# A hybrid decoder layer on one core: the attention output's halves added on the vector engine, its turns and scalings staged, and filler, loads and splits spread

## The chip, the cores and the metric

The kernel runs on one core of a Trainium2 chip. A core has engines that run side by side, each with its own instruction queue in program order: TensorE (PE, matrix products; PEld is its load of the stationary operand), the vector engine (DVE), the scalar engine (ACT), GpSimd (POOL) and SyncE (SP, which here issues every DMA). Matrix products and transposes write to PSUM, which has eight banks of 128 x 512 fp32 values; the other operands lie in SBUF. The metric is the device time of one execution in microseconds, taken as the median over runs.

## The reference

One layer on x of 1024 tokens by 1024 columns, all in fp32:

```
h   = rmsnorm(x) * g_pre;  p = h @ W_in                      (1024 x 3584)
A   = attention, 8 heads of 64: three dilated windows (128,1), (512,4), (2048,16),
      mixed per position by their softmax denominators, ALiBi bias, causal
R   = HGRN2 recurrence, 4 heads of 128, per-head norm, output gate silu
x   = x + rmsnorm(concat[rmsnorm(A), R] @ W_out) * g_post
x   = x + rmsnorm(relu(rmsnorm(x) @ W1)^2 @ W2) * g_mlp_post  (4096 wide)
```

The mixture of the three windows is the same as one causal softmax whose bias has the logarithm of the number of windows that contain the key; this bias comes as a table for each head.

## The kernel before, in words

Products that need fp32 precision are made of three passes over pairs of reduced-precision values (`three_pass`, lines 86 to 89): every operand is split into a high part (an ACT copy, line 83) and a low part (a DVE subtraction, line 84). The order of all instructions on every engine is written out by hand.

**Recurrence.** After the first norm and turns (to about 45 us), `hgrn_core` runs for the four heads: a diagonal from `prod` (`pd`, line 379), seven levels of a chunk tree (`pl`, line 393), a state update, and the output `po` in two groups of four blocks (lines 434 to 446). These steps are too short for TensorE, so matmuls of the next projection are put between them.

**Filler.** A projection is a generator that yields a cost after each handful of matmuls (650 after three 128x512 ones, 330 after three 128x256 ones). `fill(ns)` runs the generators of a queue until that much cost is spent, and an overshoot is kept as a credit. `drain()` runs all that is left.

**Attention.** The eight heads are taken in four pairs. `attn_proj(pr)` makes q, v and k of a pair: two halves of 512 tokens each, 48 units of 650 and two of 450, 32,100 in all. For k it copies a high part (ACT), subtracts a low part (POOL, line 524) and copies both to the other 64 partitions by four DMAs for each half. There are 64 steps, (head, block b of 128 rows), b = 0 to 7. Step s issues: the exponentials of step s+1; the scores of step s+2 (`ps`, lines 563 and 564), with bias and row maximum on the DVE (line 566); the turns of step s (`pt`, line 590), split by ACT (line 593) and DVE (line 594); and after every second step `weigh` for a group of 256 rows.

`weigh` (from line 600) multiplies the stacked high and low halves of v with the turned probabilities. So the upper and lower 64 partitions of its bank `po` (tag `pv`, two banks; the trace says `pov`) hold two halves of the result which have to be added. ACT copies them to `ot`. One step later `finish` multiplies `ot` by `fold`, two 64 x 64 unit matrices on top of each other (line 618): one fp32 product adds the halves and turns them. The DVE then scales rows by the reciprocal denominators into `anat` (line 621). A pair's `anat` is stored to DRAM; the last pair's stays.

After the scores and turns a step asks for filler: `fill(2700.0 - 320.0 * b)`, in the last 16 steps 1300. The K part of the next pair waits until step 6 of the pair before it. Two steps ahead of a new pair (`fresh`) all that is left of the projection is drained, since the next scores need it.

**Bridge to the output projection.** `hooks` adds work to single steps. From 45: gain and the recurrence's rows of the first four blocks are loaded (`early_open`, `erows`, into blocks that hold the layer's input until the last projection is done), POOL multiplies them (line 658), TensorE turns them (`pmt`, line 698), and splits of W_out are made at steps 46 to 49. `early_out` then is filler. Rows of the attention part are loaded at 55, normed at 59 to 62.

**Output projection and second norm.** The loop over t = 0 to 7 makes the product with W_out, the residual and the second norm, and `next_turn(t - 2)` turns the result for the next layer; for t - 2 = 0 to 3 it also splits it (`h2`), ACT and DVE reading PSUM. After it come the two layers of the second half as Strassen-like products, which fill the time from about 660 us to the end.

## Time and profile before

| What | us |
|---|---|
| median of three runs | 1316.15 (1313.2 to 1319.82) |
| the profiled execution | 1313.2 |
| its span, first to last instruction | 1311.4 |
| PE busy | 1264.5 (96%) |
| DVE busy | 858.7 (65%) |
| ACT busy | 515.1 (39%) |
| POOL busy | 283.6 (22%) |

A row of a group has the line, engine, operation, output and inputs, shape and count; then the busy time, the mean of one instruction in ns, and the idle time of its engine just before. A row of waits has who waited for whom, the total, how often, and the longest. In the table of stretches the last three numbers are the granted TensorE clock (1.00 is full speed), the busy share of the DMA engines and GB/s. Ends of matmuls are modelled and overlap, so the pace is read from starts, not from durations.

### The profile page before, as it was taken

To read this page: it belongs to the slowest core of one execution; us is meant where nothing else is said; L and a number is where in the kernel's file an instruction comes from. 1 tells how busy PE (TensorE), PEld (TensorE's weight loads), DVE (VectorE), ACT (ScalarE), POOL (GpSimd) and SP (SyncE) were. 2 spreads that over 40 slices of the span, in tenths; PEclk is the share of its full clock that TensorE was granted. 3 is DMA by queue.
4 is the path that set the end of the run, shared out by engine and by line. 5 is a ranking of instruction groups with operands and counts; after the bars stand their busy time and mean duration, and the time that the engine had idled before them with its cause. 6 is when DMAs were issued, how large, how long until landed. Compare 5 with 4: busy or idle time off the path is not lost. (4 is left out here: it accounts for less than half of the span.)

```text
span 1311.4 us, 17500 instructions
## 1 busy us (share of the span) xinstructions
PE 1264.5 (96%) x6730; PEld 1081.8 (82%) x6730; DVE 858.7 (65%) x1431; ACT 515.1 (39%) x908; POOL 283.6 (22%) x276
## 2 busy tenths in 40 slices
PE   9999999999989999898999899999999999999997
PEld 8898989888878888786887688888887888888886
DVE  5556566675656655666757656666666777688956
ACT  6612121213545554564555422222234633344412
POOL 0000000012011111123432178755651000000002
PEclk9999999999999999899999899999999999999999
DMA  5202020213122222416251444534469453444423
GB/s 203 65 17 65 17 64 17 65 49 98 48 81 65 81 65 59 137 41 215 97 177 58 143 168 169 177 129 140 174 222 347 165 196 115 146 131 128 147 80 130
DMA packets 58563, 153.77 MB, mean 117 GB/s; under 512 B 5104, under 2 KB 13040, under 8 KB 58224
## 3 DMA queue, kind: packets, MB, share of 16 engines
q1 hardware_dynamic: 58480, 152.66, 34.9%
q8 instruction: 53, 0.87, 0.3%
q14 instruction: 30, 0.25, 0.1%
HBM read 106.50 MB, written 39.85 MB: 112 GB/s over the span
## 5 line engine op out<-in xcount | busy, mean ns | idle before, releaser
L88 PE MATMUL f<-bl,ah 128*128 128x512 f32 x392 | 152.6, 389 | 0.5 <-DVE bl L84 0.5
L87 PE MATMUL f<-bh,ah 128*128 128x512 f32 x392 | 152.6, 389 | 0.4 <-ACT acc L1441 0.4
L89 PE MATMUL f<-bh,al 128*128 128x512 f32 x392 | 152.5, 389 | 0.0
L84 DVE TENSOR_TENSOR al<-ar,ah 128x1024 fp32r<-128x1024 f32 x49 | 60.7, 1239 | 49.6 <-ACT ah L83 21.7
L88 PEld LDWEIGHTS f<-bl,ah 128*128 128x128 f32 x392 | 73.6, 188 | 16.1 <-DVE bl L84 0.8
L87 PEld LDWEIGHTS f<-bh,ah 128*128 128x128 f32 x392 | 73.6, 188 | 16.0 <-ACT acc L1441 0.9
L89 PEld LDWEIGHTS f<-bh,al 128*128 128x128 f32 x392 | 73.6, 188 | 15.3
L83 ACT ACTIVATE ah<-ar 128x1024 fp32r<-128x1024 f32 x49 | 52.3, 1067 | 54.1 <-PE f L89 25.3
L566 DVE CUSTOM_DVE_ANT_0 p<-ps,bt 128x512 f32<-128x512 f32 (+2 forms) x96 | 50.6, 552 | 31.7 <-PE ps L564 31.5
L1577 POOL TENSOR_SCALAR fp<-fss 128x1 f32<-128x1 f32 x8 | 3.5, 432 | 268.8 <-ACT fd L1574 268.8
L594 DVE TENSOR_TENSOR ptl<-pt,pth 128x512 fp32r<-128x512 f32 (+2 forms) x96 | 50.2, 551 | 16.4 <-ACT pth L593 16.3
L593 ACT ACTIVATE pth<-pt 128x512 fp32r<-128x512 f32 (+2 forms) x96 | 43.3, 486 | 42.0 <-PE pt L590 41.8
L590 PE MATMUL pt<-ident,p 128*128 128x128 f32 x288 | 43.6, 279 | 11.6 <-DVE ptl L594 11.6
L393 PEld LDWEIGHTS pl<-qt,kt 128*128 128x128 f32 x448 | 52.9, 192 | 1.5 <-PE pm_av L89 0.9
L393 PE MATMUL pl<-qt,kt 128*128 128x64 f32 x448 | 53.5, 272 | 0.5 <-DVE qt L399 0.5
L577 ACT ACTIVATE p<-p,nm 128x128 f32<-128x128 f32 (+3 forms) x64 | 49.5, 773 | 10.0 <-DVE nm L572 5.7
L524 POOL TENSOR_TENSOR kl<-kf,kh 64x512 fp32r<-64x512 f32 x16 | 20.4, 1274 | 151.3 <-ACT kh L523 150.7
L231 ACT ACTIVATE inat<-pig,rstd 128x128 f32<-128x128 f32 x32 | 11.6, 367 | 95.4 <-PE pig L89 82.3
L590 PEld LDWEIGHTS pt<-ident,p 128*128 128x128 f32 x288 | 33.7, 142 | 17.2 <-DVE ptl L594 14.2
L83 ACT ACTIVATE bh<-br 128x1024 fp32r<-128x1024 f32 x28 | 29.9, 1067 | 41.1 <-PE f L89 35.8
L79 POOL TENSOR_SCALAR ms<-hss 128x8 f32<-128x8 f32 x4 | 0.8, 196 | 203.6 <-DVE hss L445 203.6
L84 DVE TENSOR_TENSOR wl<-raw,wh 128x1024 fp32r<-128x1024 f32 x23 | 31.3, 1359 | 18.0 <-ACT wh L83 18.0
(1584 smaller groups left out, 3848.9 us busy)
## 6 DMA issues: line engine op xcount, KB each, us to landing
ar<-actd SPq DMA_DIRECT2D x49, 512.0 KB, 3.7
raw<-in_w_in_dram SPq DMA_DIRECT2D x28, 512.0 KB, 3.7
w1r<-in_w_ff_dram SPq DMA_DIRECT2D x14, 1024.0 KB, 6.5
br<-in_w_ff_dram SPq DMA_DIRECT2D x14, 1024.0 KB, 6.5
actd<-e SPq DMA_DIRECT2D x17, 768.0 KB, 4.2
actd<-e SPq DMA_DIRECT2D x11, 1024.0 KB, 4.1
xr<-in_x_dram SPq DMA_DIRECT2D x8, 512.0 KB, 9.0
bt<-in_bias_tab_dram SPq DMA_DIRECT2D x8, 512.0 KB, 4.3
```

The lines of the kernel that those rows point to most:

```text
L83: S.activation(hi, src, AF.Copy)
L84: eng.tensor_tensor(out=lo, in0=src, in1=f32(hi), op=ALU.subtract)
L87: TE.matmul(dst, lhs[0], rhs[0], start=start, stop=False)
L88: TE.matmul(dst, lhs[0], rhs[1], start=False, stop=False)
L89: TE.matmul(dst, lhs[1], rhs[0], start=False, stop=stop)
L393: TE.matmul(pl[:, n * 64:(n + 1) * 64], kt[:, n * P:(n + 1) * P], qv[:, n * nb:(n + 1) * nb, 1, :], start=True, stop=True)
L524: G.tensor_tensor(out=stacks[i]["kl"][a:b, sl], in0=full[a:b], in1=f32(stacks[i]["kh"][a:b, sl]), op=ALU.subtract)
L566: V.tensor_tensor_reduce(out=pe[:, k0:k0 + n], in0=pS[:, :n], in1=bts[hd][:, o:o + n], scale=1.0, scalar=-3.0e38, op0=ALU.add, op1=ALU.max ...
L577: S.activation(pe[:, :nk], pe[:, :nk], AF.Exp, bias=nm[:, b:b + 1], accum_out=dn[:, b:b + 1])
L590: TE.transpose(pt[:, j * P:(j + 1) * P], pe[:, jj * P:(jj + 1) * P], ident)
L593: S.activation(hi, src, AF.Copy)
L594: V.tensor_tensor(out=lo, in0=src, in1=f32(hi), op=ALU.subtract)
```

## The change

Six things, all between the recurrence and the second half.

1. *Halves.* `fold` and its load go. `weigh` has ACT copy one half of `po` straight into the 64 partitions of `anat` that belong to the head. `finish_step`, called once a step, moves a result through three stages: the DVE adds the other half from PSUM; for the second head of a pair, TensorE turns the two heads' 128 x 256 together by two transposes into the free half of the bank; the DVE scales by the reciprocals of both heads at once (`rd` now has a column for each head) back into `anat`.
2. *Filler in attention.* `3400 - 360 b` up to step 43, 1000 to step 47, 1300 after. A pair's projection counts as done before its last yield; at a `fresh` step only what the next scores need is run.
3. *Rows' load.* `early_rows` is called in the last pair's K projection after its first half. It loads rows and a separate copy of the gain; POOL's products move to steps 45 and 46, turns to 47 to 50, `early_out` starts at 48. The last head's bias table shares a tile with the gain. Norms and gains of the attention rows come at 61 to 63.
4. *Filler in the recurrence.* 4500 before `pd` become 2200 before and 2300 after it; 3000 after `po` become 1500 between the two groups and 1500 after.
5. *Second layer's input parts.* `next_turn` only copies; `split_tokens` splits two blocks at once from that copy in SBUF at t = 4 and t = 6.
6. W_out's second part takes slabs, the third the rotating buffers.

```diff
-        fill(4500 * scale)
+        fill(2200 * scale)
         pd = bank("t", f"pd{h}")
...
         cur = tot
+        fill(2300 * scale)
...
             pos.append(po)
+            if g4 == 0:
+                fill(1500 * scale)
...
-        fill(3000 * scale)
+        fill(1500 * scale)
...
+            if hf == 0 and pr == AH // 2 - 1:
+                early_rows()
             full = half(f"kf{pr}{hf}")
...
+            pairs[pr] = (stacks, vs)
             yield 650.0
-        pairs[pr] = (stacks, vs)
...
-        ot = sp.tile([P, 256], F32, tag="ot", name=f"ot{hd}_{g}", bufs=1)
-        S.activation(ot, po[:, :256], AF.Copy)
-        return po, ot
+        a, b = halves[hd % 2]
+        S.activation(turned_of(hd, g)[a:b], po[a:b, :256], AF.Copy)
+        return po
+    def finish_step(*new):
+        for hd, g, po in stages[2]:
+            scale_rows(hd, g, po)
+        for hd, g, po in stages[1]:
+            ft = turned_of(hd, g)
+            for u in range(2):
+                TE.transpose(po[:, 256 + u * P:256 + (u + 1) * P], ft[:, u * P:(u + 1) * P], ident)
+        for hd, g, po in stages[0]:
+            a, b = halves[hd % 2]
+            c, d = halves[1 - hd % 2]
+            o = turned_of(hd, g)[a:b]
+            V.tensor_tensor(out=o, in0=po[c:d, :256], in1=o, op=ALU.add)
+        stages[:] = [list(new), [x for x in stages[0] if x[0] % 2], stages[1]]
+    def scale_rows(hd, g, po):
-        for u in range(2):
-            TE.matmul(po[:, 256 + u * 64:256 + (u + 1) * 64], ot[:, u * P:(u + 1) * P], fold, start=True, stop=True)
-        for u in range(2):
-            b = 2 * g + u
-            V.tensor_scalar(anats[pr][:, b, hd % 2], po[:, 256 + u * 64:256 + (u + 1) * 64],
-                            stats[hd]["rd"][:, b:b + 1], None, op0=ALU.mult)
+        V.tensor_tensor(out=anats[pr][:, 2 * g:2 * g + 2], in0=po[:, 256:].rearrange("p (u i d) -> p u i d", u=2, i=2),
+                        in1=stats[hd]["rd"][:, 2 * g:2 * g + 2].unsqueeze(3).to_broadcast([P, 2, 2, 64]), op=ALU.mult)
...
+    def early_rows():
+        early["rows"] = wide.tile([P, NE, AW], F32, tag="A", name="erows")
+        early["table"] = wide.tile([P, 2, T], F32, tag="A", name="etable")
...
+        gains["early"] = early["table"][:, 1, :AW]
+        nc.sync.dma_start(out=gains["early"], in_=g_mix[:AW].partition_broadcast(P))
+        for q in range(NE // 2):
+            nc.sync.dma_start(out=early["rows"][:, 2 * q:2 * q + 2],
+                              in_=mix_dram[2 * q * P:2 * (q + 1) * P, :AW].rearrange("(n p) d -> p n d", p=P))
...
-            if th == 0:
-                hi, lo = (q[:, :, c:c + P] for q in h2[kh])
-                split_into(hi, lo, src)
+    def split_tokens(kh, c):
+        hi, lo = (q[:, :, c:c + 2 * P] for q in h2[kh])
+        split_into(hi, lo, hraw[kh, 0][:, :, c:c + 2 * P])
...
     hooks = {
-        45: lambda: [drain(), load_gain("gmix", "R", g_mix), early_open()],
-        46: lambda: w_get(WO0, 0),
-        47: lambda: [w_get(WO0 + 1, 0), row_rec(0), row_rec(1)],
-        48: lambda: [row_turn(0, 0), w_get(WO0 + 2, 0), row_rec(2), row_rec(3)],
-        49: lambda: [row_turn(1, 0), w_get(WO0 + 3, 0), queue.extend(early_out(t) for t in range(NE))],
-        50: lambda: row_turn(2, 0),
-        51: lambda: row_turn(3, 0),
+        45: lambda: [row_rec(0), row_rec(1)],
+        46: lambda: [w_get(WO0, 0), row_rec(2), row_rec(3)],
+        47: lambda: [row_turn(0, 0), w_get(WO0 + 1, 0), load_bias(AH - 1)],
+        48: lambda: [drain(), load_gain("gmix", "R", g_mix), early_sums(), w_get(WO0 + 2, 0), row_turn(1, 0),
+                     queue.extend(early_out(t) for t in range(NE))],
+        49: lambda: [w_get(WO0 + 3, 0), row_turn(2, 0)],
+        50: lambda: row_turn(3, 0),
...
-        59: lambda: [row_norm(0), row_gain(0)],
-        60: lambda: [row_norm(1), row_gain(1)],
-        61: lambda: [row_turn(0, 1), w_get(WO0 + 4, 0)],
-        62: lambda: [row_norm(2), row_gain(2), w_get(WO0 + 5, 0)],
-        63: lambda: w_get(WO0 + 6, 0),
+        61: lambda: [row_norm(0), row_gain(0), w_get(WO0 + 4, 0)],
+        62: lambda: [row_turn(0, 1), row_norm(1), row_gain(1), w_get(WO0 + 5, 0)],
+        63: lambda: [row_norm(2), row_gain(2), w_get(WO0 + 6, 0)],
     }
...
         if fresh and s + 2 < n_steps:
-            drain()
+            while pairs[(s + 2) // 16] is None:
+                fill(1.0)
             if (s + 2) // 16 + 1 < AH // 2:
+                drain()
                 queue.append(attn_proj((s + 2) // 16 + 1))
             look(s + 2)
...
-        fill(2700.0 - 320.0 * b if s < n_steps - 16 else 1300.0)
+        fill(3400.0 - 360.0 * b if s < n_steps - 20 else 1000.0 if s < n_steps - 16 else 1300.0)
...
+        if t in (4, 6):
+            for kh in range(2):
+                split_tokens(kh, (t - 4) * P)
```

## The prediction

> **What bounds the kernel now.** I read the page first (shares), then the table of stretches by stage, then TensorE's own waits, then the timeline round the longest of them, then the granted clock there.

> ```profile
> span 1311.4 us, 17500 instructions
> PE 1264.5 (96%) x6730; PEld 1081.8 (82%) x6730; DVE 858.7 (65%) x1431; ACT 515.1 (39%) x908; POOL 283.6 (22%) x276
> ```

> TensorE is the bound: 96% busy, the next engine 65%. So two things count: TensorE work that goes away, and the 47 us in which TensorE stands. The stages (stretch, length, busy time of PE, PEld, DVE, ACT, POOL, granted clock, DMA share, GB/s):

> ```profile
> 60.00:320.00 260.00, 258.61 (x1779) 238.36 (x1778) 160.06 (x288) 56.91 (x94) 18.41 (x16) 1.00 0.17 49
> 320.00:392.00 72.00, 64.94 (x386) 56.02 (x385) 44.90 (x143) 36.39 (x82) 10.21 (x8) 1.00 0.26 74
> 392.00:460.00 68.00, 64.14 (x377) 56.12 (x376) 40.50 (x131) 34.66 (x76) 10.26 (x8) 0.96 0.25 70
> 460.00:533.00 73.00, 65.35 (x381) 56.94 (x380) 39.73 (x131) 34.41 (x77) 12.30 (x10) 0.94 0.29 87
> 533.00:590.00 57.00, 55.76 (x348) 49.40 (x347) 39.27 (x119) 38.84 (x90) 10.82 (x18) 0.97 0.21 61
> 590.00:662.00 72.00, 67.01 (x330) 54.46 (x330) 49.66 (x69) 37.89 (x103) 27.42 (x57) 1.00 0.44 152
> ```

> TensorE stands 1.4 us in the recurrence (60 to 320), 7.1, 3.9 and 7.7 us in the first three attention pairs, 1.2 in the last, 5.0 in output projection and second norm (590 to 662). Its waits, over the whole run (total, times, longest, in us):

> ```profile
> PE pt L590 <- DVE ptl L594: 11.6, 7, 2.8
> PE pmt L698 <- POOL erows L658: 4.7, 1, 4.7
> PE ps L563 <- DVE mx L566: 2.3, 1, 2.3
> PE ph L785 <- DVE esum L775: 2.3, 1, 2.3
> PE pmt L698 <- DVE row L682: 1.5, 1, 1.5
> PE pmt L698 <- DVE ptl L594: 0.9, 1, 0.9
> PE pwo L87 <- ACT mt L83: 0.8, 1, 0.8
> ```

> In attention TensorE waits for the DVE to split the turned probabilities, although the DVE is busy 54 to 69% there: single steps are uneven, not the totals. The end of the second pair in the timeline:

> ```profile
> 449.18 0.69 DVE L521 TENSOR_TENSOR kf<-pm_ak,rrow 128x512 f32<-128x512 f32 x1 [4.75 <-PE pm_ak L89]
> 450.80 1.04 PE L590 MATMUL pt<-ident,p 128*128 128x128 f32 x8
> 451.68 0.56 PE L618 MATMUL pov<-fold,ot 128*128 128x64 f32 x4
> 452.30 2.00 DVE L84 TENSOR_TENSOR wl<-raw,wh 128x1024 fp32r<-128x1024 f32 x1 [2.04 <-ACT wh L83]
> 455.49 0.48 PE L590 MATMUL pt<-ident,p 128*128 128x128 f32 x1 [2.85 <-DVE ptl L594]
> ```

> The rest of the next pair's projection is drained in one lump; the DVE is idle for 4.75 us, then gets everything at once, and TensorE, whose filler is spent, stands 2.85 us. The clock answers to such places:

> ```profile
> 382.80:386.20 3.40, 1.89 (x16) 1.57 (x15) 1.85 (x1) 2.85 (x6) 2.40 (x2) 1.00 0.51 118
> 451.00:454.50 3.50, 1.64 (x14) 1.32 (x12) 2.20 (x2) 2.59 (x6) 2.14 (x2) 1.00 0.53 124
> 454.50:461.30 6.80, 5.81 (x22) 5.34 (x23) 2.83 (x13) 1.86 (x6) 0.00 (x0) 0.50 0.54 169
> 519.30:522.70 3.40, 1.47 (x13) 1.22 (x12) 1.33 (x4) 2.67 (x6) 2.26 (x2) 1.00 0.51 116
> 522.70:526.20 3.50, 3.50 (x18) 3.31 (x18) 2.92 (x12) 3.06 (x8) 0.00 (x0) 0.51 0.92 238
> 529.60:536.40 6.80, 4.12 (x17) 3.83 (x18) 2.09 (x2) 2.50 (x6) 4.96 (x4) 0.50 0.20 80
> ```

> After 3.4 us in which TensorE worked 1.64 or 1.47 us the clock is halved; after 1.89 us it is not. Half of what ran in such a stretch is lost: 2.9 us in the first, 2.1 in the last; the middle one ends in the 4.7 us wait for POOL anyway and costs nothing.

> **The change part by part.** Groups by shape within 320 to 590 that price it (busy us, mean ns, idle before):

> ```profile
> L594 DVE TENSOR_TENSOR ptl<-pt,pth 128x512 fp32r<-128x512 f32 x48 | 32.3, 687 | 14.0 <-ACT pth L593 14.0
> L566 DVE CUSTOM_DVE_ANT_0 p<-ps,bt 128x512 f32<-128x512 f32 x48 | 32.3, 686 | 27.9 <-PE ps L564 27.9
> L618 PE MATMUL pov<-fold,ot 128*128 128x64 f32 x128 | 18.6, 270 | 0.0
> L621 DVE TENSOR_SCALAR anat<-pov,rd 128x64 f32<-128x64 f32 x62 | 14.2, 271 | 0.0
> L610 ACT ACTIVATE ot<-pov 128x256 f32<-128x256 f32 x32 | 12.3, 384 | 20.4 <-PE pov L607 20.0
> L84 DVE TENSOR_TENSOR wol<-raw,woh 128x1024 fp32r<-128x1024 f32 x5 | 6.9, 1376 | 1.7 <-ACT woh L83 1.7
> L594 DVE TENSOR_TENSOR ptl<-pt,pth 128x256 fp32r<-128x256 f32 x16 | 6.7, 416 | 1.5 <-ACT pth L593 1.5
> ```

> *1, fold matmuls out.* 64 fp32 products with `fold` are 128 instructions. Four of them move TensorE's end from 451.84 to 452.24: 0.40 us, by 32 groups 12.8 us. In come 32 transposes (two for each pair of heads and group of 256 rows); the row of eight takes 1.04 us with its first latency, eight start before 451.68, so 0.11 us each: 3.5 us. Net -9.3; by the groups' busy time, which counts latency, 18.6 - 32 x 0.15 = 13.8 is the other end. I take -9.3, the pace, since TensorE works without a break there.

> *2, DVE and ACT of it.* Out: 64 scalings, 14.7 us. In: 32 additions of 64x256 and 16 scalings of 128x256 from PSUM, at the 416 ns of a 128x256 operation: 20.0 us. The DVE gets 5.3 us more over 270 us in which it idles over 100; hidden at the even steps, counted in the budgets below. ACT's 32 copies keep their length, with half the partitions. Queued behind the new DVE additions is only the next step's work; they run a step after the copy they need, so no new wait is seen. The store of a pair's output goes two steps later, past one weight load on SP, and is read four steps after at the earliest; the load of `fold` at the start goes: 0.

> *3, filling.* A projection is 32,100 units of cost. Steps ask for 25,280 a pair now (so some 6,800, ten units, go as the lump) and for 34,240 after, so the lump vanishes and the last two steps of a head get 1240 and 880 in place of 780 and 460. What waits instead: at the step with seven turns before a new pair the queue is empty. There the DVE has 2 x 686 + 687 + 416 + 2 x 416, with small ones 3.8 us, TensorE four score matmuls and six turns, 1.6: a wait of some 1.6 at two borders, since one step of slack lies before it. In the steps that carry splits of W_out (46 and 47, filler spent) the DVE has 3.3 (0.5 for a score, 687 and some 550 for turns, 0.15, 1376) and 5.1 (0.6, 2 x 687, 0.15, 2 x 416, 1376, and 687 for a row), TensorE 2.5 and 1.6: 4.2 of wait. The first steps have 0.8 us more filler against the 2.3 wait: 1.5 left. A half-clock stretch after step 47, chance one half: 1.5. Small ones in the middle of pairs: 1.1. After: 2 x 1.6 + 4.2 + 1.5 + 1.5 + 1.1 = 11.5. Before, from the rows above: 11.6 + 4.7 + 2.3 + 0.9 of waits and 5.0 of clock, 24.5. Net -13.0. Bounds: -24.5, if all waits go; +2, if each lump only becomes as long a wait elsewhere.

> *4, rows' load.* Rows and a copy of the gain are loaded as soon as the first half of the last K projection has read its blocks, before that half's four copies on the SP queue; POOL multiplies them at steps 45 and 46. The 4.7 wait is in part 3. What stands behind them on SP, the K copies, isn't needed for three steps: 0. `row_norm` and `row_gain` of rows 0 and 1 come two steps later, the first only a step before its turn; and at the end a turn takes a PSUM bank that the new scaling frees. I take +1.0 for both, between 0 and the 2.85 of the longest wait.

> *5, recurrence.* 2300 of the 4500 units before `pd` move behind it, half of the last 3000 between its two groups. What covers `prod`:

> ```profile
> 130.04 0.39 PE L89 MATMUL pm_f<-hTh,wl 128*128 128x512 f32 x1
> 130.26 0.28 PE L87 MATMUL pig<-wig2h,hTh 128*128 128x256 f32 x1
> 130.38 0.28 PE L88 MATMUL pig<-wig2l,hTh 128*128 128x256 f32 x1
> 132.95 0.69 DVE L369 TENSOR_TENSOR prod<-qt,kt 128x512 f32<-128x512 f32 x1
> ```

> `prod` ends 3.2 us after the last `pm_f`. 2200 units are seven of 330, each three matmuls at 0.12: 2.5 us. So `pd` waits 0.7 in three heads, 0.5 in the last (four units of 650 are 2.8 us): +2.7, where nothing is gained, because the stage stands 1.4 us in all. Bounds 0 to 3.

> *6, second layer's input parts.* Eight splits of 128x512 (half of them ACT, half DVE) leave the steps of t = 2 to 5, four of twice that length come at t = 4 and 6.

> ```profile
> 616.10 0.69 DVE L84 TENSOR_TENSOR h2l<-ph,h2h 128x512 fp32r<-128x512 f32 x1 [1.84 <-ACT h2h L83]
> 617.08 0.69 DVE L84 TENSOR_TENSOR h2l<-ph,h2h 128x512 fp32r<-128x512 f32 x1 [0.28 <-ACT h2h L83]
> 617.68 1.28 DVE L775 SCALAR_TENSOR_TENSOR esum<-xres,x2r,gmlp 128x1024 f32<-128x1024 f32 x1
> ```

> `esum`, for which TensorE then waits 2.3, is held by these two and their 1.84 and 0.28 of idling; without them it starts some 3 us earlier. The 2.3 and the 0.8 go: -3.1. The later lumps are two DVE operations of about 1.24, in steps without a TensorE wait above 0.4 us: 0. Bounds -5 to +2.

> Sum: -9.3 - 13.0 + 1.0 + 2.7 - 3.1 = -21.7. The profiled execution took 1313.2 us (span 1311.4), so 1291.5; it was the fastest of the three shown, 2.95 under their median, against which I forecast 1316.15 - 21.7, rounded 1294.

> [...] Row first: of the 1.64 us of work ahead of the first half-clock stretch, the eight turns that start at 450.80 are nearly 0.9. [...]

> **Rivals.**
> *A, the waits stay.* TensorE's saving falls in steps where it waits for the DVE, and parts 3 and 4 only move waits. For it: all 11.6 us of `pt` waits are for the DVE, whose work grows by 5.3. Against: the 4.75 idle before the 2.85 wait. Then -9.3 and about half of the clock loss, -2.5, remain: 1304.
> *B, the clock.* Turns and pauses together bring a half-clock stretch at each of four borders: 4 x 2.9 = 11.6 where I count 1.5: 10 later, 1304. For it: 1.64 us and 1.89 us lie close; against: the waits left are shorter. [...]
> *C, slower.* A PSUM bank of `pov` is now held until the third stage has scaled it, and two serve all. If each of the 16 held banks makes the next weighing wait for the DVE's queue, the change loses as soon as one costs over 21.7/16 = 1.36 us; at the 2.85 of the longest wait it gives +24, 1340. For it: the steps leave one step between scaling and reuse. Against: TensorE waits for the DVE at `pov` only 0.2 us now, and the scaling comes directly behind a split that it needs anyway.
> *D, nothing.* The lump was no loss, as the work must be done, and new waits on the additions eat the fold's 9.3: 1316.

> **How the numbers follow.** Forecast 0.62, A 0.16, B 0.08, C 0.06, D 0.08. The three runs lie 0.5% apart (6.6 us), about what can be told from no change. Faster by more: forecast, A, B, 0.86; same: D, 0.08; slower: C, 0.06. Range: part 3's lower bound reaches 1283; upward A and B with their 1304 and 5 us of spread, 1309; that leaves out D and C, and some of the bottom.

> **What would show it.** TensorE's busy time down by 9 to 14; in the attention stage no DVE idling of 4.7 before `kf`, `pt` waits under 6 in sum, no wait on `erows`; half-clock stretches there down from three to one at most. A new wait of `pd` on the DVE of 0.5 to 0.8 in each head. No `ph` wait on `esum`. Wrong would be: waits of `pov` for the scaling (C), `pt` waits as before at other steps (A), clock under 0.95 in every pair (B).

## The result, and the profile after

The changed kernel takes 1308.98 us in the median (1306.96 to 1309.98) against 1314.61 of the kernel before beside it. The ratio is 0.9946, with a 95% interval of 0.9930 to 0.9962: 5.6 us faster by the medians, where 21.7 were forecast. The profiled execution took 1308.3 us.

Its page, first lines (after):

```profile
span 1306.5 us, 17279 instructions
PE 1254.8 (96%) x6634; PEld 1070.6 (82%) x6634; DVE 866.9 (66%) x1411; ACT 518.7 (40%) x904; POOL 282.9 (22%) x276
```

TensorE's busy time fell by 9.7 us, as forecast (9 to 14), but the span by 4.9 only. To see where the rest went, both spans are cut at the same points of the work: the last `po` of the recurrence, the fifth step's first turn of the last head, the first `ph` turn, the first product of the second layer. The table of stretches of the kernel before (stretch, length, busy time of PE, PEld, DVE, ACT, POOL, granted clock, DMA share, GB/s):

```profile
0.00:316.31 316.31, 311.31 (x2124) 285.77 (x2125) 191.11 (x352) 94.30 (x176) 19.21 (x22) 1.00 0.20 64
316.31:571.33 255.02, 236.31 (x1390) 206.03 (x1389) 153.90 (x502) 133.73 (x297) 37.81 (x32) 0.97 0.26 75
571.33:607.32 35.99, 34.89 (x198) 29.70 (x196) 21.92 (x44) 21.63 (x55) 13.51 (x28) 1.00 0.54 181
607.32:671.84 64.52, 59.53 (x298) 48.57 (x296) 44.61 (x60) 32.65 (x89) 23.54 (x49) 1.00 0.32 111
```

The same of the changed kernel:

```profile
0.00:320.80 320.80, 313.67 (x2124) 287.63 (x2125) 190.82 (x352) 93.99 (x176) 18.70 (x22) 0.99 0.20 63
320.80:564.50 243.70, 225.61 (x1303) 194.11 (x1302) 160.35 (x485) 136.96 (x294) 37.60 (x30) 0.99 0.28 80
564.50:606.48 41.98, 34.90 (x188) 29.11 (x186) 23.62 (x45) 22.14 (x56) 15.58 (x29) 0.96 0.47 155
606.48:667.61 61.13, 59.24 (x298) 48.69 (x296) 44.72 (x56) 32.76 (x85) 21.31 (x49) 1.00 0.33 114
```

| Stretch | change of length, us | forecast |
|---|---|---|
| to the end of the recurrence | +4.5 | +2.7 |
| attention up to the last half head | -11.3 | about -21.4: 29 of the 32 groups of fold, and the filling's -13.0 |
| last half head to the first `ph` turn | +6.0 | +0.1: the rest of fold, and +1.0 |
| output projection and second norm | -3.4 | -3.1 |
| second half (the remainder) | -0.7 | 0 |

In attention TensorE is 10.7 us less busy, but it stands 243.70 - 225.61 = 18.1 us, after 18.7 before: the waits that were to go did not. In the short stretch behind it TensorE is as busy as before and stands 7.1 us in place of 1.1. By the span 4.9 us came of the 21.7: of the 16.8 that are missing, 10.1 lie in attention, 5.9 at its end and 1.8 in the recurrence, and the two last rows give back 1.0. TensorE's waits (total, times, longest), after:

```profile
PE pt L592 <- DVE ptl L596: 10.3, 6, 3.0
PE ps L565 <- DVE mx L568: 4.1, 3, 1.4
...
PE pmt L725 <- DVE anat L640: 3.5, 1, 3.5
...
PE pov L609 <- DVE anat L640: 2.1, 3, 1.7
PE pd L377 <- DVE prod L367: 2.0, 2, 1.0
PE pmt L725 <- issue: 1.9, 2, 1.2
PE pmt L725 <- DVE ptl L596: 1.9, 1, 1.9
```

The 4.7 us on `erows` and the 2.3 on `esum` are gone, though TensorE still stands 1.9 us in two pieces at the turns of `erows` (the row `pmt <- issue`, for which the profile names no other engine). The turns still wait 10.3 us in sum (11.6 before). The scores wait 1.4 us in each of three pairs, where one wait of 2.3 stood. Two kinds are new: the first `pd` products of two heads, and at the end the waits for `anat`, the scaling of the three stages.

**The wait at a pair's end.** It is 3.04 us, three times. From the timeline of the changed kernel at the first of them (start, length, engine, line, what, idle before):

```profile
376.69 0.69 DVE L524 TENSOR_TENSOR kf<-pm_ak,rrow 128x512 f32<-128x512 f32 x1 [1.04 <-PE pm_ak L88]
...
377.42 1.28 ACT L526 ACTIVATE kh<-kf 64x512 fp32r<-64x512 f32 x2 [1.98 <-DVE kf L524]
...
378.73 1.04 ACT L579 ACTIVATE p<-p,nm 128x896 f32<-128x896 f32 x1
...
379.89 0.87 ACT L595 ACTIVATE pth<-pt 128x512 fp32r<-128x512 f32 x2
...
380.52 1.02 DVE L596 TENSOR_TENSOR ptl<-pt,pth 128x512 fp32r<-128x512 f32 x2 [1.67 <-ACT pth L595]
```

TensorE's turns go on at 381.26, when the first `ptl` is done. The projection's last unit was spent a step too early, and then four pieces of work stand in a row: `kf` on the DVE, its two copies on ACT ahead of the exp, the exp, the split. The prediction budgeted this step with the DVE's work alone (3.8 us, of which 1.6 would show); the DVE idles for 1.67 us in it. ACT's order is the chain.

**The end.** The timeline of the changed kernel from the last scores to the output projection:

```profile
585.13 1.23 DVE L83 TENSOR_TENSOR wol<-raw,woh 128x1024 fp32r<-128x1024 f32 x1 [1.61 <-ACT woh L82]
...
586.28 0.42 DVE L640 TENSOR_TENSOR anat<-pov,rd 128x256 f32<-128x256 f32 x1
...
586.72 0.42 DVE L635 TENSOR_TENSOR anat<-pov,anat 64x256 f32<-64x256 f32 x1
...
586.84 0.63 PE L725 MATMUL pmt<-ident,row 128*128 128x128 f32 x4 [3.48 <-DVE anat L640]
```

Row 1's turn takes a bank of `pv`. This bank is free once the scaling has read it, and the scaling stands behind the last split of W_out on the DVE, which waits 1.61 us for its ACT copy. TensorE has nothing else and stands 3.48 us.

**The clock.** In the profile of the changed kernel the granted clock is 0.50 from 137.60, 448.21, 516.48, 588.16 and 738.35 us, for 3.41 us each, and from 1301.54 to the end; in that of the kernel before from 454.47, 529.57 and 741.19 for 6.83 us each, from 522.74 for 3.41 and from 1307.81 to the end. In the rest the two records, which begin at 7.9 and 7.3 us, have 1.00, and in each all these changes lie a multiple of 3.41 us apart. Stretches of 3.4 us of the changed kernel, laid between such multiples:

```profile
134.20:137.60 3.40, 2.46 (x21) 2.37 (x21) 3.30 (x6) 0.67 (x1) 0.00 (x0) 1.00 0.00 0
...
376.50:379.90 3.40, 1.72 (x11) 1.28 (x9) 2.12 (x6) 2.41 (x5) 1.70 (x2) 1.00 0.18 42
379.90:383.30 3.40, 2.04 (x17) 2.00 (x18) 2.54 (x7) 2.97 (x6) 0.82 (x1) 1.00 0.73 146
...
444.80:448.20 3.40, 0.42 (x4) 0.18 (x2) 1.70 (x7) 3.33 (x7) 2.52 (x2) 1.00 0.50 115
448.20:451.60 3.40, 3.34 (x16) 3.34 (x17) 2.37 (x8) 1.78 (x4) 0.00 (x0) 0.50 0.63 191
```

The waits at the first and second pair's end are equally long. At the first, the multiples cut the wait in two, the stretches hold 1.72 and 2.04 us of work, and the clock stays at 1.00; at the second, one stretch holds nearly all of it, with 0.42 us of work, and the next 3.4 us run at 0.50 (1.7 us lost). The same happens at the third border (0.58 us of work from 513.10 to 516.50, then 0.50) and once at the end (1.36 us from 584.80 to 588.20, then 0.50). The first row is the recurrence's: 2.46 us of work, and 0.50 from 137.60 all the same; the last section comes back to it.

### The profile page after: what moved, and what is told of

It is laid out like the page before. It is cut to its first block, busy times and chain, and to the rows that moved or that the text cites. A ratio compares the mean times of both kernels' runs of the same rounds, so it can differ in the third digit from the quotient of the medians.

```text
span 1306.5 us, 17279 instructions
## 1 busy us (share of the span) xinstructions
PE 1254.8 (96%) x6634; PEld 1070.6 (82%) x6634; DVE 866.9 (66%) x1411; ACT 518.7 (40%) x904; POOL 282.9 (22%) x276
## 5 line engine op out<-in xcount | busy, mean ns | idle before, releaser
L87 PE MATMUL f<-bl,ah 128*128 128x512 f32 x392 | 152.6, 389 | 0.5 <-DVE bl L83 0.5
L88 PE MATMUL f<-bh,al 128*128 128x512 f32 x392 | 152.5, 389 | 0.0
L83 DVE TENSOR_TENSOR al<-ar,ah 128x1024 fp32r<-128x1024 f32 x49 | 60.7, 1238 | 50.0 <-ACT ah L82 19.6
L87 PEld LDWEIGHTS f<-bl,ah 128*128 128x128 f32 x392 | 73.6, 188 | 15.8 <-DVE bl L83 0.8
L88 PEld LDWEIGHTS f<-bh,al 128*128 128x128 f32 x392 | 73.6, 188 | 15.2
L568 DVE CUSTOM_DVE_ANT_0 p<-ps,bt 128x512 f32<-128x512 f32 (+2 forms) x84 | 44.4, 553 | 16.9 <-PE ps L566 16.4
L592 PE MATMUL pt<-ident,p 128*128 128x128 f32 x288 | 44.1, 282 | 10.3 <-DVE ptl L596 10.3
L229 ACT ACTIVATE inat<-pig,rstd 128x128 f32<-128x128 f32 x32 | 11.7, 367 | 97.2 <-PE pig L88 84.2
L527 POOL TENSOR_TENSOR kl<-kf,kh 64x512 fp32r<-64x512 f32 x16 | 20.4, 1274 | 137.3 <-ACT kh L526 136.7
L592 PEld LDWEIGHTS pt<-ident,p 128*128 128x128 f32 x288 | 34.5, 145 | 14.7 <-DVE ptl L596 12.2
L396 DVE TENSOR_TENSOR kt<-kt,tot 128x512 f32<-128x512 f32 x28 | 20.2, 721 | 35.8 <-PE pl L392 35.8
```

Of the source, the lines that this page charges most:

```text
L83: eng.tensor_tensor(out=lo, in0=src, in1=f32(hi), op=ALU.subtract)
L87: TE.matmul(dst, lhs[0], rhs[1], start=False, stop=False)
L88: TE.matmul(dst, lhs[1], rhs[0], start=False, stop=stop)
L527: G.tensor_tensor(out=stacks[i]["kl"][a:b, sl], in0=full[a:b], in1=f32(stacks[i]["kh"][a:b, sl]), op=ALU.subtract)
L568: V.tensor_tensor_reduce(out=pe[:, k0:k0 + n], in0=pS[:, :n], in1=bts[hd][:, o:o + n], scale=1.0, scalar=-3.0e38, op0=ALU.add, op1=ALU.max ...
L592: TE.transpose(pt[:, j * P:(j + 1) * P], pe[:, jj * P:(jj + 1) * P], ident)
```

## The experiments

Ratios are to the kernel before, run beside each on the same chip; 1.0000 of it is about 1316 us, so 0.001 is 1.3 us. The changed kernel has 0.9946 (0.9930 to 0.9962).

**Each part undone, and part 1 alone.** The recurrence undone:

```diff
-        fill(2200 * scale)
+        fill(4500 * scale)
         pd = bank("t", f"pd{h}")
...
-        fill(2300 * scale)
...
-            if g4 == 0:
-                fill(1500 * scale)
...
-        fill(1500 * scale)
+        fill(3000 * scale)
```

> The changed kernel with the recurrence's filling put back (4500 units ahead of the diagonal products, none behind them, 3000 before the gate), everything else as changed. Theory (the recurrence now costs 4.0 us: its diagonal products wait for the DVE's product in heads 1 and 2, and the clock is halved once behind the first of them): 4 us less than the changed kernel, so about 9.5 us (0.7%) under the kernel before, the two waits on prod under 0.2 us and no half-clock stretch before 320 us. Rival (these waits only take the place of others later on): within 1 us of the changed kernel.

Measured: 1303.11 us, ratio 0.9898 (0.9875 to 0.9921), 6.3 us under the changed kernel. The `pd` waits are gone. The theory holds in its direction, with 6.3 us by the times where it said 4.0; the two intervals allow some 3 to 10. One of its signs fails: a half-clock stretch came ahead of 320 us all the same, at 269.9, behind `pd` products that did not wait. With one such stretch in either profile, the recurrence ends 2.7 us earlier than in the changed kernel (318.07 for 320.80), and the first pair takes 1.1 less.

The attention stage's filling undone:

```diff
-            while pairs[(s + 2) // 16] is None:
-                fill(1.0)
-            if (s + 2) // 16 + 1 < AH // 2:
-                drain()
+            drain()
+            if (s + 2) // 16 + 1 < AH // 2:
...
-        fill(3400.0 - 360.0 * b if s < n_steps - 20 else 1000.0 if s < n_steps - 16 else 1300.0)
+        fill(2700.0 - 320.0 * b if s < n_steps - 16 else 1300.0)
```

(with hooks 45 to 51, the rows' load and the order of W_out's slabs as before)

> The changed kernel with the attention stage's filling, the drain at a pair's end, the place of the rows' load and the hooks of steps 45 to 51 as in the kernel before; halves and stages, recurrence and the second layer's input parts as changed. By the prediction the undone part was worth 13 us, so this would be 12 to 13 us slower than the changed kernel, 7 slower than the kernel before. Theory (the lumps before a pair's end have only become waits of 3 us and half-clock stretches elsewhere, so the part is worth nothing): within 3 us of the changed kernel. Rival (it costs): 3 us or more faster than the changed kernel.

Measured: 1316.71 us, ratio 1.0001 (0.9983 to 1.0020), 7.2 us slower than the changed kernel, and the intervals of the two allow some 4 to 10. So the part does work, at about half of its 13 us; the theory that it is worth nothing falls.

The second layer's input parts undone:

```diff
             S.activation(hraw[kh, th][:, :, c:c + P], src, AF.Copy)
+            if th == 0:
+                hi, lo = (q[:, :, c:c + P] for q in h2[kh])
+                split_into(hi, lo, src)
...
-        if t in (4, 6):
-            for kh in range(2):
-                split_tokens(kh, (t - 4) * P)
```

> The changed kernel with the second layer's input parts split as in the kernel before: eight pieces of 128x512 in the steps of rows 0 to 3 in place of four lumps at rows 4 and 6. By the prediction 3.1 us slower than the changed kernel; by the marks on TensorE's timeline, where the output stage gained 1.8 us, 1.8 slower, with the wait of ph on esum back at about 2 us. Rival (something else shortened that stage, the lumps cost as much as they save): within 1 us of it.

Measured: 1314.13 us, ratio 0.9988 (0.9971 to 1.0005), 5.5 us slower than the changed kernel, and the intervals of the two allow 2 to 9. The stretch that the part touches, from the first `ph` turn on, in this kernel:

```profile
608.60:673.13 64.53, 60.36 (x297) 49.60 (x296) 44.59 (x60) 32.69 (x89) 23.53 (x49) 0.97 0.33 111
```

It is as long as before (64.52), and 61.13 with the part. Here 2.3 of the 3.4 us are standing (the 2.2 on `esum` above all), and the rest goes with a half-clock stretch that the kernel before does not have (a clock of 0.97 in this row, 1.00 there). Against the kernel before the part takes standing alone away, 4.99 to 1.89 us: the 3.1 of the forecast.

Part 1 alone, in the kernel before:

```diff
-        for i, g, a in last_fold:
-            finish(i, g, *a)
+        finish_step(*weighed)
...
-        59: lambda: [row_norm(0), row_gain(0)],
-        60: lambda: [row_norm(1), row_gain(1)],
+        61: lambda: [row_norm(0), row_gain(0), w_get(WO0 + 4, 0)],
+        62: lambda: [row_turn(0, 1), row_norm(1), row_gain(1), w_get(WO0 + 5, 0)],
```

> The kernel before with part 1 alone: the fold products replaced by DVE additions, turns of both heads together and scaling, three stages, and the two-step later norms of rows 0 and 1 that these need. By the prediction -9.3 + 1.0: 8.3 us (0.63%) under the kernel before. Theory now: TensorE's pace falls by 9 to 12 us as forecast, but the end of the attention stage loses 3.4 of it in waits for the scaling and for the PSUM banks that it holds: 6 to 8.5 under. Rival (the DVE's extra 5 us lands in the steps that already wait for it, and eats most of it): 0 to 4 us under.

Measured: 1320.35 us, ratio 1.0043 (1.0025 to 1.0061): 5.7 us slower than the kernel before, outside of every expectation. Its waits and its two stretches (attention up to the last half head, then to the first `ph` turn):

```profile
PE pt L590 <- DVE ptl L594: 14.7, 9, 3.1
...
PE pmt L715 <- DVE anat L638: 3.3, 1, 3.3
```

```profile
316.60:569.91 253.31, 230.25 (x1297) 196.79 (x1297) 160.63 (x485) 134.99 (x294) 37.52 (x30) 0.95 0.25 76
569.91:614.12 44.21, 37.86 (x193) 31.38 (x192) 23.72 (x45) 22.24 (x56) 15.61 (x29) 0.92 0.43 148
```

TensorE's work falls: 6.1 us less busy time in attention, although the mean clock is lower there (0.95 for 0.97) and so its work takes longer; 8.4 of the fold's 9.3 were forecast for this stretch. But it stands 253.31 - 230.25 = 23.1 us there in place of 18.7, and the end takes 44.21 us in place of 35.99. Part 1 by itself makes time elsewhere: 4.4 us of waits in attention, more half-clock stretches (a clock of 0.95 and 0.92 in the two rows, where the kernel before has 0.97 and 1.00), and 8.2 us at the end.

**Part 1 with the other parts in place.** The last pair's halves folded by TensorE again, in the changed kernel (two small constants moved to make room for `fold`):

```diff
+        if hd // 2 == AH // 2 - 1:
+            ots[hd, g] = sp.tile([P, 256], F32, tag="ot", name=f"ot{hd}_{g}", bufs=1)
+            S.activation(ots[hd, g], po[:, :256], AF.Copy)
+            return po
...
         for hd, g, po in stages[0]:
+            if (hd, g) in ots:
+                fold_rows(hd, g, po)
+                continue
```

(with norms and gains at steps 59, 60 and 62 again)

> The changed kernel with part 1 undone for the last pair of heads alone (its halves folded by TensorE and scaled one step later, as in the kernel before; norms and gains of rows 0 to 2 at steps 59, 60 and 62 again); the small constants g_pre and the gate's bounds moved into another tile to make room. Theory (the end of the attention stage pays for the three stages: between the last head's fifth step and the first ph turn the changed kernel loses 6.0 us to the kernel before): those 6 us come back, 2.3 of TensorE pace are lost (8 groups by 0.40 - 0.11), net 3 to 4 us faster than the changed kernel. Rival (the 6 us are lost to the order of the splits of W_out and the gains, whatever forms the rows): 2 us slower.

Measured: 1305.41 us, ratio 0.9926 (0.9910 to 0.9943), 2.6 us under the changed kernel by the ratios. The intervals overlap, but the place is clear in the trace:

```profile
569.66:604.70 35.04, 33.62 (x191) 28.73 (x190) 22.00 (x44) 21.42 (x54) 13.57 (x28) 1.00 0.57 183
```

The end is back at 35.0 us, from 42.0. The stretch begins 5.2 us later than in the changed kernel (569.66 for 564.50). Of these 1.5 are lost in the recurrence, which the edit leaves alone, in a profile with one half-clock stretch more there; 3.7 are lost in attention, where there is one more too, and where folding costs TensorE time again; the mean clock of the profiled execution is 0.988, for 0.992. The run undoes the late norms together with the three stages, so it doesn't tell the two apart.

All pairs folded, and only the last one folded, both with the recurrence undone:

```diff
-        if hd // 2 == AH // 2 - 1:
+        if True:
             ots[hd, g] = sp.tile([P, 256], F32, tag="ot", name=f"ot{hd}_{g}", bufs=1)
```

> The changed kernel without the recurrence's new filling and with part 1 undone for all four pairs: every pair's halves folded by TensorE and scaled a step later. To be held against the kernel with the recurrence undone alone (1303.1 us) and the next one, in which only the last pair folds. By the prediction's price of part 1, 0.29 us of TensorE pace for each of 32 groups, it is 9.3 us slower than it should be with part 1 and an end that costs nothing, and 7 us slower (24 groups) than the kernel in which only the last pair folds. Rival (in the first three pairs the time saved falls into waits for the DVE, as in the run with part 1 alone, which stood 1.4 us ahead after three and a half pairs): within 2 us of that kernel.

> Both repairs that gained by themselves: the recurrence's filling as before, and the last pair's halves folded as before, the rest as changed. If they add: 5.9 + 2.6 us under the changed kernel, 0.988 of the kernel before, about 1300. If the second only moves a wait: 1303, as with the recurrence alone.

Measured: 1302.47 us, 0.9905 (0.9875 to 0.9934), and 1298.14 us, 0.9869 (0.9840 to 0.9897). The two repairs add, as expected. With the recurrence undone and all four pairs by part 1 it is 0.9898: so part 1 as a whole is worth 0.9905 - 0.9898, about 1 us with an interval of some 5 to either side, in three pairs 4.7 and in the last pair -3.8 by the middle values. The 4.7 lie between the price (7) and the rival (within 2), and the times can't decide. The attention stretch of the first of these kernels, then of the second:

```profile
317.18:563.09 245.91, 234.25 (x1394) 204.97 (x1394) 154.15 (x502) 135.43 (x297) 37.88 (x32) 0.99 0.27 79
```

```profile
317.19:560.73 243.54, 227.84 (x1323) 196.50 (x1322) 159.69 (x490) 136.79 (x297) 37.91 (x32) 0.99 0.27 80
```

This is the cleanest pair of rows: the same clock, the same filling. Three pairs of part 1 take 6.4 us of TensorE work away (forecast: 24 groups by 0.29, 7.0), and TensorE stands 15.7 us in place of 11.7. So 2.4 us are left of the 6.4 in this stretch; nearly two thirds become waits. (The rest of the difference of the times is not there: the two profiles differ by 3.1 us behind the first `ph` turn, which the edit leaves alone.) TensorE's waits for the turns' split, with all pairs folded, then with only the last one:

```profile
PE pt L591 <- DVE ptl L595: 7.2, 4, 2.5
```

```profile
PE pt L591 <- DVE ptl L595: 9.2, 6, 3.0
```

These rows and the wait of the scores (2.7 for 1.8) hold 2.9 of the 4.0 us: the saving falls into waits for the DVE, which at a pair's end is the last of the chain shown above. The first row of the stretches shows also what the filling does without part 1: 18.7 us of standing fall to 11.7, and the stretch to 245.9 from 255.0, 9.1 us of the 13.0.

**The recurrence alone, in the kernel before** (the edit of part 4 of the change, on the kernel before):

> The kernel before with the recurrence's new filling alone (2200 units ahead of the diagonal products, 2300 behind, 1500 and 1500 round the second half of the outputs). By the prediction +2.7 us; by the two marks of the changed kernel's trace, where the stage lost 4.0 us in two waits of 1.0 and a half-clock stretch, +4; by the difference of the runs with and without it, +5.9. Rival (what it moves to the later steps shortens a wait there): 0.

Measured: 1315.57 us, ratio 0.9997 (0.9979 to 1.0014): it costs nothing there, the rival. The trace shows where the cost comes back. From the start of attention to the last turn of its second head, in the kernel before and in this one:

```profile
316.31:383.89 67.58, 63.37 (x373) 54.62 (x372) 41.67 (x136) 36.38 (x77) 10.74 (x9) 1.00 0.22 63
```

```profile
321.15:385.92 64.77, 63.07 (x372) 54.56 (x372) 41.78 (x136) 36.28 (x77) 10.80 (x9) 1.00 0.23 66
```

The recurrence ends 4.8 us later (321.15 for 316.31), but TensorE's standing in the next pair falls from 4.2 to 1.7 us: filler that the recurrence no longer spends at its end is there for this pair's waits. In the changed kernel the steps ask for more filler than there is, which is likely why nothing comes back there: the same work takes 65.9 us, and 64.7 with the recurrence undone. That is an interaction of the filling in attention with that of the recurrence (the prediction's items 3 and 5), which the prediction did not have.

**The end's order.** Two runs. In the first, gains go ahead of norms, the last splits behind the scalings, and row 1's turn takes a bank of the turns; in it the norm is taken of rows already multiplied by the gain, so it leaves out the right norm.

```diff
-        61: lambda: [row_norm(0), row_gain(0), w_get(WO0 + 4, 0)],
+        61: lambda: [row_gain(0), row_norm(0), w_get(WO0 + 4, 0)],
...
-    w_get(WO0 + 7, 0)
     x_again(0)
     finish_step()
-    row_turn(1, 1, True)
+    w_get(WO0 + 6, 0)
+    row_turn(1, 1)
     finish_step()
+    w_get(WO0 + 7, 0)
```

> The changed kernel with the order of its end alone changed: row_gain ahead of row_norm at steps 61 to 63 (so POOL multiplies while ACT squares), the splits of the last two blocks of W_out behind the additions and the scaling of the last groups, and the turn of row 1 in a bank of the turns in place of one that the scaling holds. Theory (the waits of pmt and pov of 1.9, 1.7 and 3.5 us and the half-clock stretch behind them are this order): 4 to 7 us faster than the changed kernel. Rival (they come back as waits for the late parts of W_out): within 1.5 us of it.

Measured: 1308.01 us, ratio 0.9941 (0.9919 to 0.9963): no gain that can be told, though its stretch up to the first `ph` turn takes 39.2 us in place of 42.0. The second has the end's order without the gains, on the kernel with the recurrence undone:

> The kernel with the recurrence undone, and the end's order changed in two places: the splits of the last two blocks of W_out behind the last additions and scalings, and row 1's turn in a bank of the turns. Norms and gains stay in the changed kernel's order. Theory (the 3.5 us wait at row 1's turn is these two; in the run with the gains moved too, the stretch up to the first ph turn was 2.8 us shorter): 2 to 4 us faster than the kernel with the recurrence undone alone (1303.1). Rival: within 1 us of it, the wait returning at the late parts of W_out.

Measured: 1301.09 us, ratio 0.9895 (0.9872 to 0.9918), where the kernel without the edit has 0.9898. By the times nothing is shown. In its trace the place changes as the theory says:

```profile
568.25:607.02 38.77, 33.84 (x188) 27.81 (x186) 23.53 (x45) 21.99 (x56) 14.66 (x29) 1.00 0.49 169
```

38.8 us in place of 42.0, the 3.5 us wait gone; so by this trace about half of the end's 6.0 is this order. The waits of 1.9 and 1.7 us stay as they were, one at a row's turn and one at the bank of `weigh`; that the late norms cause the first is likely, but not shown by itself.

**The bank that a group holds.** The turned halves in a bank of the turns:

```diff
+            tb = turned_banks[hd, g] = bank("t", f"pft{hd}_{g}")
             for u in range(2):
-                TE.transpose(po[:, 256 + u * P:256 + (u + 1) * P], ft[:, u * P:(u + 1) * P], ident)
+                TE.transpose(tb[:, u * P:(u + 1) * P], ft[:, u * P:(u + 1) * P], ident)
```

> The changed kernel with the recurrence undone, all pairs' halves added by the DVE, and the turned halves written to a bank of the turns in place of the group's own: a pov bank is then free after the addition, one to two steps earlier. To be held against the kernel with the recurrence undone alone (1303.1). Theory (at the end, pov waits 1.7 us and row 1's turn 3.5 us for banks that the scaling frees): 4 to 6 us faster. Rival (what was waited for is the DVE's queue, whichever bank): within 1.5 us, or slower by new waits of the turns for their two banks.

Measured: 1322.99 us, ratio 1.0062 (1.0041 to 1.0084), some 20 us slower than the kernel that it is held against. Its waits:

```profile
PE pt L589 <- DVE ptl L593: 19.5, 13, 3.3
PE pft L629 <- DVE ptl L593: 4.9, 5, 2.1
```

The two banks of the turns have no room: the new turns wait for a `ptl` five times, and the turns `pt` wait 13 times in place of 6. The place that the change chose, the free half of the group's own bank, is by far the better one.

**The filler at a pair's end.** First less filler a step, then the same with two units of the next projection ahead of the new scores:

```diff
-        fill(3400.0 - 360.0 * b if s < n_steps - 20 else 1000.0 if s < n_steps - 16 else 1300.0)
+        fill(3250.0 - 350.0 * b if s < n_steps - 20 else 1000.0 if s < n_steps - 16 else 1300.0)
```

> The changed kernel with 3250 - 350 b units of filler in a step in place of 3400 - 360 b, nothing else: a pair asks for 32,400 in place of 34,240, so two units of K's projection are left for the step at which TensorE now waits 3.0 us at each pair's end, and kf's copies no longer stand ahead of that step's exp on ACT. Theory (the three waits and two half-clock stretches come from spending the filler one step early): the waits fall below 1 us each, 6 to 10 us faster than the changed kernel. Rival (the chain kf, kh, exp, pth, ptl only moves a step on, to the next pair's first scores): within 2 us of it.

> As the evened kernel, and the first two units of the next projection go ahead of the new pair's first scores at a pair's end, in place of behind them. If the evened kernel waits there for the K copies, this covers about 1.4 us at each of the first two borders: 2 to 3 us faster than the evened kernel. If it doesn't wait there: the same within 1 us.

Measured: 1309.07 us, 0.9951 (0.9934 to 0.9967), and 1310.10 us, 0.9958 (0.9938 to 0.9978): both as the changed kernel. The first one's waits:

```profile
PE ps L565 <- DVE mx L568: 6.1, 3, 2.0
PE pt L592 <- DVE ptl L596: 5.6, 5, 1.4
...
PE pmt L725 <- issue: 3.6, 2, 2.9
```

The single waits of 3.0 are gone, but 1.2 and 1.4 stand in the steps after, the scores wait 2.0 in place of 1.4, and the sum of these three rows is 15.3 after 16.3. Spreading the same filler otherwise moves the wait; it does not shorten the chain. No wait for the copies of K shows at the new scores, so for the second run "the same" was named, and so it came, 0.9 us apart; in its trace single waits of 3.0 and 2.6 at a pair's end are back.

Then the chain itself: the exp of the step after next is issued ahead of the twelfth step's filler, so `kf`'s copies come behind it on ACT. It stands on the kernel with both repairs.

```diff
+        if s % 16 == 12 and s < n_steps - 16:
+            raise_(s + 2)
         hooks.get(s, lambda: None)()
```

> The kernel with both repairs, and at the twelfth step of each of the first three pairs the exp of the step after next is issued ahead of that step's filler, so that the copies of kf no longer stand before it on ACT. Theory (the 3.0 us wait at a pair's end is the chain kf, two copies of 1.28 together, exp, copy, subtraction): the waits fall by 1.3 us each and the half-clock stretches behind them get rarer, 4 to 7 us faster than the kernel with both repairs (1298.1). Rival (the DVE's own work at that step, scores and subtractions, is as long): within 1.5 us of it.

Measured: 1295.69 us, ratio 0.9848 (0.9827 to 0.9868), against 0.9869 without it; the span of the profiled execution is 4.3 us shorter. The waits of the turns, 9.2 us in six without it (the row above), are with it:

```profile
PE pt L591 <- DVE ptl L595: 6.9, 6, 1.9
```

The longest waits lose 1.2 us, about the exp's length (1.04, and 0.19 for its sum): the exp leaves the chain, which is the mechanism. The attention stretch falls from 243.54 to 239.78 us, with one half-clock stretch less; the mean clock of the profiled execution is 0.995, for 0.992. By the times the gain is 2.8 us where 4 to 7 were expected, and it lies inside the intervals, so that the time gains is likely and not shown. This kernel is 1.5% faster than the kernel before and 1.0% faster than the changed one, and beats both.

**The clock.** Eight products that nobody reads, put into the wait at a pair's end:

```diff
+        if s % 16 == 13 and s < n_steps - 16:
+            spare = bank("mm", f"warm{s}")
+            own = pairs[hd // 2][0][hd % 2]
+            for _ in range(8):
+                TE.matmul(spare, own["q"][:, :P], own["kh"][:, :512], start=True, stop=True)
```

Measured: 1296.19 us, ratio 0.9869 (0.9829 to 0.9909), the same ratio as without them. In the trace no half-clock stretch is left between 208 and 727 us, where the kernel without the products has two, and the mean clock of the profiled execution is 0.995 in place of 0.992: so the stretches behind these waits are gone, as the theory says. Attention takes 240.70 us in place of 243.54; but by the times the gain can't be told from none.

## Why the prediction was wrong

The sign was right, but the change gave a quarter of the forecast. The step that failed first is the pricing of waits in attention, "no new wait is seen" and "a wait of some 1.6 at two borders": each took the DVE's work alone, where a chain over ACT and the DVE sets when TensorE goes on. The turns' waits, of which under 6 us were to stay, are 10.3. The second is the price of the end, +1.0, where 6.0 came. Step by step, by the prediction's items:

1. *Fold matmuls out, -9.3 by the pace.* Right. Three pairs took 6.4 us of busy time away where 7.0 follow from the forecast's 0.29 us a group. (That price took modelled ends, 451.84 to 452.24; by the starts round the same four products, 451.68 to 452.04, it is 0.36 - 0.11 = 0.25 us, or 6.0.)
2. *DVE and ACT of it, hidden.* The durations were right, below: 422 ns for an addition and 406 for a scaling, where 416 were taken; ACT's copies of 64x256 took 379 ns, those of 128x256 before 384. What failed is "no new wait is seen". Part 1 alone adds 4.4 us of standing in attention; with the filling in place three pairs add 4.0. The forecast had argued with the DVE's idle share over 270 us. In the steps with waits, TensorE's end is set by a chain over ACT and the DVE, and there work taken from TensorE is turned into a wait.

```profile
L635 DVE TENSOR_TENSOR anat<-pov,anat 64x256 f32<-64x256 f32 x32 | 13.5, 422 | 0.7
L640 DVE TENSOR_TENSOR anat<-pov,rd 128x256 f32<-128x256 f32 x16 | 6.5, 406 | 0.0
```

3. *Filling in attention, -13.0.* Mis-sized: 9.1 us in the trace without part 1, 7.2 by the times of the changed kernel. The step that failed is "a wait of some 1.6 at two borders": it is 3.04 at three, because I budgeted the DVE alone and not ACT's row of copies, exp and copies. The two lumps of half clock at borders, 1.7 each, were counted at half of one, the 1.5 after step 47. The 1.64 us of work, read there from 3.5 us that lie across the change of the clock at 454.47, are 1.59 in the 3.41 us ahead of it (451.05 to 454.46).
4. *Rows' load and late norms, +1.0.* The rows' load was nearly right: 1.9 us at its turns in place of 4.7. The end, with the late norms and the bank held, was the worst term: +6.0 us in the changed kernel, +8.2 with part 1 alone, above its bound of 2.85. I took the bound from the longest wait before; but three waits of 1.9, 1.7 and 3.5 us follow each other, and a half-clock stretch follows (0.50 from 588.16 to 591.57).
5. *Recurrence, +2.7.* The mechanism was right, the places weren't: `pd` waits 0.94 and 1.01 us in two heads, not in the first and the last. In the changed kernel's profile the recurrence ends 4.5 us later, two waits of 1.0 and a half-clock stretch (0.50 from 137.60 to 141.01). Taken out of the changed kernel it gives 6.3 us by the times; put into the kernel before, nothing. Some of the difference is the filler that comes back in the next pair, some may be the clock behind `pd`, which from 72.90 to 79.70 us is 1.00 in one profile and 0.50 in another of the same recurrence (last section); how it divides is not shown.
6. *Second layer's input parts, -3.1.* Right: -3.4, of which 3.1 are waits.

Of the rivals, A has the mechanism: the waits stay, and TensorE's saving falls into them. Its time does not come out; the change of 5.6 us lies midway between its 12 and D's nothing, and D's new waits are there in part. C's mechanism is there too, as 1.7 and 3.5 us for banks that the scaling frees, but at the end alone. B's half-clock stretches are there at two borders, not four.

What stays open: why the times of part 3's and part 5's removal differ from the traces by 2 us each. The half-clock stretches lie at other places of the work in each of the two profiles (the first from 454.47 us in the kernel before, from 137.60 in the changed one) and cost 1.7 us for each 3.41, which is of this size, but this was not separated. The new order of W_out's parts (the change's sixth part) was not run alone.

## What to carry to other kernels

Work taken off the bounding engine counts only in steps that this engine ends; in steps that end with another engine's chain it becomes a wait, here nearly two thirds of it. So price such a step by the whole chain over all engines in issue order, not by the busy share of one, and look last at the place where the pipeline drains, where the added stages cost 6.0 us here. Undo the parts of a change one at a time: here two of them cost more than they gave, and without them the same idea gives 1.3 to 1.5%.

## What was not expected of the hardware

**A clock that stays behind a stretch of turns.** Four stretches of the kernel with the attention's filling undone, and the turns' share of the third:

```profile
339.70:343.10 3.40, 1.43 (x6) 0.78 (x5) 3.36 (x7) 1.73 (x6) 0.88 (x1) 1.00 0.52 98
343.10:346.50 3.40, 3.40 (x12) 2.56 (x11) 3.25 (x11) 2.82 (x5) 0.00 (x0) 0.51 0.55 167
384.10:387.50 3.40, 1.51 (x13) 1.19 (x11) 2.00 (x2) 2.81 (x6) 2.26 (x2) 1.00 0.50 116
387.50:390.90 3.40, 1.45 (x10) 1.29 (x11) 3.27 (x13) 0.88 (x3) 0.00 (x0) 1.00 0.95 304
```

```profile
384.10:387.50 3.40, 1.03 (x8) 0.89 (x8) 0.00 (x0) 1.09 (x2) 1.00 0.50 116
```

The first stretch has 1.43 us of work in six instructions (0.24 each), and in the second the clock is 0.51. The third has 1.51 us, of which up to 1.03 are eight turns (0.13 each), and in the fourth the clock is 1.00. Without its turns the third holds about 0.5 us, a third of what the first has, and yet the clock was halved behind the first and not behind the third. The busy time with the turns in it doesn't sort every case either: in the kernel before, the 3.41 us up to 454.46 hold 1.59 us, 0.79 of them turns, and from 454.47 the clock is 0.50.

**A half clock behind 2.46 us of work.** In the changed kernel the stretch from 134.2, shown above, holds 2.46 us of busy time, and the clock is 0.50 from 137.60 to 141.01. The 128x1 products of `pd` are this much of it:

```profile
134.20:137.60 3.40, 1.14 (x9) 0.97 (x8) 0.16 (x1) 1.00 0.00 0
```

Without them 1.32 us are left, less than the 1.43 behind which the clock was halved above; that these products make the difference is not shown by a run. In the kernel with the end's order alone, whose recurrence is that of the kernel before, the clock is 0.50 for 6.8 us behind the first `pd`:

```profile
72.90:79.70 6.80, 6.80 (x34) 6.80 (x34) 4.57 (x7) 0.74 (x2) 0.00 (x0) 0.50 0.10 38
```

The same 6.8 us in the kernel before:

```profile
72.90:79.70 6.80, 6.80 (x60) 6.80 (x60) 4.97 (x9) 0.74 (x2) 0.00 (x0) 1.00 0.08 29
```

It has 60 products at 1.00 where the other has 34, and its record shows 1.00 up to 454.47. So 3.4 us are lost at this head in one execution and none in the other, and a difference of 3 us between two single profiles of this kernel says nothing by itself.
